# Merge stage of a hybrid decoder block: 11 gates and w_out loaded ahead of the first tiles' stores, parts added by VectorE, next chunk's loads written behind a row block

## The chip, the cores and the metric

One core of a Trainium2 chip runs the whole program. The time is device microseconds of one execution. Engines are named as the profile names them: PE is TensorE (PEld its weight loads), DVE is VectorE, ACT is ScalarE, POOL is GpSimd, and SP is the engine whose queue (SPq) issues most DMAs. ACT issues some as well (ACTq). Each engine takes its instructions strictly in the order in which they stand.

## What is computed

One layer of a decoder block on x (1 x 2048 x 1024, float32): an RMSNorm and a projection into q, k, v, u, z and two gates; dilated windowed attention (`y_attn`, 256 wide) and a chunked spatial gating (`y_gmlp`, 512 wide); a merge; then a squared-ReLU MLP. The change is in the merge. Cut from the reference:

```python
gate_a = jax.nn.sigmoid(proj[..., GA0:GB0])
gate_b = jax.nn.sigmoid(proj[..., GB0:IN_WIDTH])
...
merged = (gate_a * jnp.einsum('bse,ed->bsd', y_attn, w_branch_attn[layer])
          + gate_b * jnp.einsum('bse,ed->bsd', y_gmlp, w_branch_gmlp[layer]))
y = jnp.einsum('bsd,de->bse', merged, w_out[layer])
x = x + _rmsnorm(y, norm_post_mix[layer])
h = _rmsnorm(x, norm_pre_mlp[layer])
```

Every product is made of three float32r products: each operand is split into a rounded part (`hi`) and the rest (`lo`), and hi x hi, hi x lo and lo x hi are summed in PSUM (`mm3`, L94). A split costs one copy by ACT (L70) and one subtraction by DVE (L78).

## The kernel before

**Stages.** The kernel first makes the projections and the attention, then the merge and the output projection, then the MLP. The merge works on four chunks of 512 positions, in the order 2, 3, 0, 1 (L900). Gates, `y_attn` and `y_gmlp` lie in device memory by then (`gate_d`, `ya_d`, `yg_d`), with the channels as rows.

**One merge** (L798) has eight steps `dt` of 128 output channels. Each step takes two gate tiles of 128x512 (g0 for the attention branch, g1 for the gMLP branch): SP loads them (L795), ACT takes the sigmoid in place (L809), PE makes the branch product (6 matmuls for g0, 12 for g1, L95 to L97, tile `b`), DVE multiplies gate and product (L813), POOL adds the two parts (L815; in the last step DVE does), and ACT and DVE split the sum into the tile `mg` (L70, L78). Products use a ring of four PSUM banks: the product of step dt+2 waits until the one of the same branch in step dt has been multiplied away. Gate tiles are rings as well: three for g0, two for g1, so a load of g1 two steps on waits for the sum of this step, and a load of g0 three steps on for its split.

**Output blocks.** After the merge of a chunk come four `out_block`s (L823) of 128 rows: 16 groups of three matmuls with the split w_out (`wo`, eight tiles), then squares, two norms and the residual on ACT and DVE (L852 to L862), and later eight transposes (tile `pt`, L868). The last block's transposes fall into the next chunk's merge, where `flush` asks for them behind step 0 and step 2. In the first block the group of the last merge step (k = 7) is moved to the eleventh place. POOL computes sums of the transposed tiles (`tt`, L873 to L876) for every second chunk.

**What is special in the first merge (chunk 2).** It runs right behind the last projection (tile `z`). `spatial_out` (L1088) is called after each step. In steps 0 and 1 it also runs `sz_out` (L425) for chunks 0 and 1: 16 small matmuls for each of four groups into the second ring of four PSUM banks (tile `sz_cg`, c the chunk, g the group, L430), a DVE instruction into a tile `sb` (L437), a product with `ur`, loaded by SP (L434), on DVE or POOL (L440), and a store of `sb` to `yg_d` by SP (L441). There are three `sb` tiles and two `ur` tiles, so the fourth group waits for the first one's store. In every step it also loads and splits one eighth of w_out (L779 to L781, `woraw`, two tiles), and after the last step it loads the two norm gains (L1099, L1100).

**The order.** Only PE's order is fixed by the code here. The orders of SP, ACT, DVE and POOL are made by a scheduler that draws them up from the order of the code and its own estimates, so that a small edit can move instructions far from it.

Of the kernel before, what the change touches and what calls it, by code (L numbers as in the profile page):

```python
# [8 lines left out]
F32 = mybir.dt.float32  # L9
# [7 lines left out]
P = 128  # L17
S = 2048
D = 1024
KT = 8  # L20
# [11 lines left out]
def bcast(src):  # L32
    return bass.AP(tensor=src.tensor, offset=src.offset, ap=[[0, P], [1, src.shape[-1]]])
# [8 lines left out]
def block_kernel(ctx, tc, a, out):  # L42
# [284 lines left out]
    with ExitStack() as e1a:  # L327
# [40 lines left out]
        for half in range(2):  # L368
# [15 lines left out]
            for n, (g, which) in enumerate(qk):  # L384
                w = nxt
# [383 lines left out]
    e2b, e2 = ExitStack(), ExitStack()  # L769
    bot = stack(e2b, "bot", 1)  # L770
    sm = stack(e2b, "sm2", 2)
    gpost = bot.tile([P, D], F32, name="gpost")
    gmlp = bot.tile([P, D], F32, name="gmlp")
    gtp = stack(e2, "gtp", 2)
    mgp = [stack(e2, "mg0", 1)]
    wop = stack(e2, "wop", 1)
    wo = [wop.tile([P, 2, D], F32R, name=f"wo{k}") for k in range(KT)]

    def load_wo(k):  # L779
        raw = bot.tile([P, D], F32, name=f"woraw{k}", tag="y1", bufs=2)  # L780
        split_in(wo[k], a["w_out"][:, k, :], raw, "act")  # L781

    def load_y(c, engs=("act", "dve")):
        cs = slice(c * 512, (c + 1) * 512)
# [3 lines left out]
        return yt  # L788

    gates = {}  # L790

    def load_gate(c, dt, wch):
        if (c, dt, wch) not in gates:
# [4 lines left out]
    def merge(c, yt, between, each=None):  # L798
        cs = slice(c * 512, (c + 1) * 512)
        mg = []  # L800
        for dt in range(KT):
            dsl = slice(dt * P, (dt + 1) * P)
            if dt % 4 == 0:
                mg.append(mgp[dt // 4].tile([P, 2, 4, 512], F32R, name=f"mg{c}{dt}", tag="mg"))
            parts = []
            for wch, ks in ((0, range(0, 2)), (1, range(2, 6))):
                load_gate(c, dt, wch)
                gt = gates.pop((c, dt, wch))
                act.activation(gt, gt, AF.Sigmoid)  # L809
# [3 lines left out]
                dve.tensor_mul(gt, gt, p)  # L813
                parts.append(gt)
            (dve if dt == KT - 1 else pool).tensor_add(parts[0], parts[0], parts[1])  # L815
# [271 lines left out]

    def spatial_out(dt):  # L1088

        nonlocal ttp  # L1090
        if dt < 2:
            sz_out(*late.pop(0))
        if dt == 1:
            ez.close()
            mgp.append(stack(e2, "mg1", 1))
            ttp = stack(e2r, "ttp", 2, side="right")
        load_wo(dt)
        if dt == KT - 1:
            sp.dma_start(gpost, bcast(a["norm_post_mix"]))  # L1099
            sp.dma_start(gmlp, bcast(a["norm_pre_mlp"]))  # L1100

# [13 lines left out]

    ttp = None
    yt = load_y(2, ("pool", "pool"))
    mg = merge(2, yt, {}, spatial_out)
    for n, c in enumerate(chunks):
        if n:  # L1120
            mg = merge(c, yt, {0: flush, 2: flush, 3: store, 6: store})
        if n < 3:
            yt = load_y(chunks[n + 1])
            for dt in range(2):
                for wch in range(2):
                    load_gate(chunks[n + 1], dt, wch)
# [578 lines left out]
```

## Time and profile before

| | us |
|---|---|
| median of 3 runs | 2776.09 (2775.97 to 2780.45) |
| the profiled execution | 2779.44 |
| its span, first to last instruction | 2777.7 |
| PE busy in the span | 2712.0 |
| merge of chunk 2 on PE (first `b` matmul to first `o` matmul) | 1132.70 to 1182.55 |
| chunk 3, first `o` matmul | 1264.55 |
| chunk 0, first `o` matmul | 1353.35 |

All times inside the span count from its start. A row of the timeline gives start, length, engine, line, operation, output tile <- input tiles, and in brackets the idle time before it and what ended that. A row of the view of waits reads: who waited, for whom, us in total, how often, the longest. A row of the view of windows gives busy us of each engine in a stretch, with the instruction count in parentheses, then the granted PE clock, the share of time the DMA engines were busy, and GB/s. Two matmuls that follow each other overlap in these rows; their pace is the distance of their starts.

### The profile page before, as it was taken

How to read it: one execution, taken by the hardware profiler on the slowest of the kernel's cores; microseconds unless marked ns; L12 is line 12 of the kernel's file. 1: busy time of each engine (PE TensorE's matmuls, PEld its weight loads, DVE VectorE, ACT ScalarE, POOL GpSimd, SP SyncE). 2: the span in 40 equal slices, each digit the busy share in tenths (PEclk: the TensorE clock that was granted, in tenths of full speed). 3: DMA queues.
4: the chain of work that ended last, by engine and by line, in shares of the span. 5: the costliest groups of instructions: out<-in, count | busy, mean ns of one | idle time of the engine just before them, and what ended most of it. 6: DMA issues, size and time to landing. Idle time of an engine off the chain costs nothing. (4 is left out here: it accounts for less than half of the span.)

```text
span 2777.7 us, 34732 instructions
## 1 busy us (share of the span) xinstructions
PE 2712.0 (98%) x12668; PEld 2242.3 (81%) x12668; DVE 1545.2 (56%) x2643; ACT 1051.9 (38%) x2151; POOL 947.3 (34%) x777
## 2 busy tenths in 40 slices
PE   9999999999999999999999999999999999999998
PEld 7888888888878887787787788878887887777787
DVE  5655552344453344554556644555436777777766
ACT  5213111244453321354444544555444333233334
POOL 0341341200000013312215432223314766677645
PEclk9999999999999999999999999999999999999999
DMA  7445455466666654655658534554343122222236
GB/s 266 168 145 169 156 152 195 126 190 195 193 217 192 190 166 149 186 190 160 183 171 268 168 103 125 181 168 126 106 146 108 54 84 84 84 84 84 84 106 213
DMA packets 298380, 426.00 MB, mean 153 GB/s; under 512 B 18528, under 2 KB 172384, under 8 KB 298208
## 3 DMA queue, kind: packets, MB, share of 16 engines
q1 hardware_dynamic: 210368, 372.12, 42.3%
q10 hardware_dynamic: 87840, 51.65, 6.2%
q8 instruction: 100, 1.64, 0.2%
q14 instruction: 72, 0.59, 0.1%
HBM read 282.99 MB, written 140.71 MB: 153 GB/s over the span
## 5 line engine op out<-in xcount | busy, mean ns | idle before, releaser
L1556 PE MATMUL ya<-T_spots,s 128*128 128x512 f32 x1272 | 313.1, 392 | 4.8 <-DVE acc L1564 2.7
L1556 PEld LDWEIGHTS ya<-T_spots,s 128*128 128x128 f32 x1272 | 239.0, 188 | 59.0 <-issue 4.5
L70 ACT ACTIVATE s<-sraw 128x768 fp32r<-128x768 f32 (+1 forms) x184 | 126.0, 695 | 358.2 <-POOL sraw L1355 199.0
L1016 PE MATMUL aa<-B,A 128*128 128x512 f32 x768 | 187.0, 396 | 6.3 <-ACT xs L1030 5.1
L78 DVE TENSOR_TENSOR s<-sraw,s 128x512 fp32r<-128x512 f32 x171 | 163.6, 979 | 34.6 <-ACT s L70 33.0
L987 POOL TENSOR_TENSOR s<-w1r 128x512 f32<-128x512 f32 x32 | 43.5, 1359 | 397.3 <-DVE S L78 337.3
L1016 PEld LDWEIGHTS aa<-B,A 128*128 128x128 f32 x768 | 145.5, 190 | 40.5 <-ACT xs L1030 6.0
L72 POOL TENSOR_SCALAR w_g<-w_g_r 128x1024 fp32r<-128x1024 f32 x32 | 34.1, 1082 | 412.3 <-PE g L97 313.7
L1556 PE MATMUL yc<-T_spots,s 128*128 128x512 f32 x624 | 164.1, 394 | 3.6 <-POOL T_spots L78 3.6
L95 PE MATMUL x<-hT_a,wq 128*128 128x512 f32 x384 | 149.7, 390 | 0.0
L97 PE MATMUL x<-hT_a,wq 128*128 128x512 f32 x384 | 149.4, 389 | 0.0
L96 PE MATMUL x<-hT_a,wq 128*128 128x512 f32 x384 | 149.4, 389 | 0.0
L1556 PEld LDWEIGHTS yc<-T_spots,s 128*128 128x128 f32 x624 | 115.8, 188 | 33.6 <-POOL T_spots L78 9.7
L653 DVE TENSOR_REDUCE o<-po 128x256 f32<-128x512 f32 x48 | 33.1, 690 | 187.5 <-PE po L652 187.5
L78 POOL TENSOR_TENSOR T_spots<-w2r,T_spots 128x512 fp32r<-128x512 f32 x86 | 123.2, 1459 | 5.4 <-ACT T_spots L70 5.4
L70 ACT ACTIVATE hl<-r 128x512 fp32r<-128x512 f32 x48 | 30.4, 633 | 233.2 <-POOL r L287 89.0
L95 PE MATMUL g<-hT_b,w_g 128*128 128x512 f32 x256 | 105.0, 410 | 0.0
L95 PE MATMUL g<-hT_a,w_g 128*128 128x512 f32 x256 | 104.8, 409 | 0.0
L95 PE MATMUL o<-wo,mg 128*128 128x512 f32 x256 | 100.8, 394 | 4.1 <-ACT mg L70 4.1
L70 ACT ACTIVATE S<-w1r 128x512 fp32r<-128x512 f32 x96 | 60.0, 629 | 112.0 <-PE ac L1016 66.6
L815 POOL TENSOR_TENSOR g<-g,g 128x512 f32<-128x512 f32 x28 | 38.8, 1385 | 185.9 <-DVE g L813 179.2
L1354 POOL TENSOR_TENSOR sraw<-sraw 128x256 f32<-128x256 f32 x56 | 41.3, 737 | 174.6 <-DVE s L78 160.3
(379 smaller groups left out, 7214.4 us busy)
## 6 DMA issues: line engine op xcount, KB each, us to landing
w1r<-in_w_mlp_in_dram SPq DMA_DIRECT2D x64, 512.0 KB, 3.6
sraw<-sd SPq DMA_DIRECT2D x128, 256.0 KB, 3.4
qk<-hl SPq DMA_DIRECT2D x24, 1024.0 KB, 5.4
qq<-qk SPq DMA_DIRECT2D x96, 256.0 KB, 5.1
w_g_r<-in_w_in_dram SPq DMA_DIRECT2D x32, 512.0 KB, 5.3
gated<-gt SPq DMA_DIRECT2D x64, 256.0 KB, 3.4
g<-gated SPq DMA_DIRECT2D x64, 256.0 KB, 4.4
w2r<-in_w_mlp_out_dram SPq DMA_DIRECT2D x16, 1024.0 KB, 6.0
```

The source lines that it names most:

```text
L70: act.activation(hi, src, AF.Copy)
L72: pool.tensor_scalar(hi, src, 1.0, 1.0, op0=OP.mult, op1=OP.mult)
L78: (pool if lo_eng == "pool" else dve).tensor_sub(lo, src, f32(hi))
L95: pe.matmul(ps, lh, rh, start=start, stop=False)
L96: pe.matmul(ps, lh, rl, start=False, stop=False)
L97: pe.matmul(ps, ll, rh, start=False, stop=stop)
L653: dve.tensor_reduce(ot[:, :, j * 64:(j + 1) * 64], po.rearrange("p (b h e) -> p b e h", b=4, h=2), axis=AX.X, op=OP.add)
L815: (dve if dt == KT - 1 else pool).tensor_add(parts[0], parts[0], parts[1])
L987: pool.tensor_add(s1, a21, a22)
L1016: pe.matmul(p, w[:, l, k, :], h[:, r, k, :], start=i in (1, 6, 5) and not k and not n, stop=k == 3 and n == 2, skip_group_check=True)
L1354: pool.tensor_add(a22, a21, a22)
L1556: pe.matmul(p, s[:, l], w[:, r], start=i in (1, 2, 5) and not m and not o, stop=m == 1 and o == 2, skip_group_check=True)
```

## The change

Four edits, all in the merge stage:

1. A new function `early_gates` stands ahead of the first merge. It writes the loads of 11 of the 16 gates of chunk 2, with the first two w_out loads among them. Six of the gates go into tiles that belong to later users (the x rows of an output block and the two norm gains); five go into the usual rings. The gains' tiles are taken only at the end of that merge.
2. w_out is loaded two steps ahead: load and split are separate, and a split asks for the load two tiles on.
3. The two parts of a step are added by DVE in every step, instead of by POOL in seven of eight.
4. The loads of the next chunk's `yt` and of its first four gates stand behind the first output block in the code, instead of ahead of it.

```diff
-    gpost = bot.tile([P, D], F32, name="gpost")
-    gmlp = bot.tile([P, D], F32, name="gmlp")
+    gpost = gmlp = None
...
     def load_wo(k):
-        raw = bot.tile([P, D], F32, name=f"woraw{k}", tag="y1", bufs=2)
-        split_in(wo[k], a["w_out"][:, k, :], raw, "act")
+        wo_raw[k] = bot.tile([P, D], F32, name=f"woraw{k}", tag="y1", bufs=2)
+        sp.dma_start(wo_raw[k], a["w_out"][:, k, :])
+
+    def split_wo(k):
+        split(wo[k][:, 0], wo[k][:, 1], wo_raw.pop(k))
+        if k + 2 < KT:
+            load_wo(k + 2)
...
+    def early_gates(c):
+
+        w = [bot.tile([P, D], F32, name=f"gates{n}", tag=t) for n, t in enumerate(("xr", "gpost", "gmlp"))]
+        places = [z[:, h * 512:(h + 1) * 512] for z in w for h in range(2)]
+        for n in range(11):
+            dt, wch = n // 2, n % 2
+            if n < 6:
+                gates[c, dt, wch] = places[n]
+                sp.dma_start(places[n], gate_d[wch * 8 + dt, :, c * 512:(c + 1) * 512])
+            else:
+                load_gate(c, dt, wch)
+            if n in (1, 3):
+                load_wo(n // 2)
...
-            (dve if dt == KT - 1 else pool).tensor_add(parts[0], parts[0], parts[1])
+            dve.tensor_add(parts[0], parts[0], parts[1])
...
-        load_wo(dt)
+        split_wo(dt)
         if dt == KT - 1:
+            gpost = bot.tile([P, D], F32, name="gpost")
+            gmlp = bot.tile([P, D], F32, name="gmlp")
...
     yt = load_y(2, ("pool", "pool"))
+    early_gates(2)
     mg = merge(2, yt, {}, spatial_out)
...
-        if n < 3:
-            yt = load_y(chunks[n + 1])
-            for dt in range(2):
-                for wch in range(2):
-                    load_gate(chunks[n + 1], dt, wch)
         for i in range(4):
             store()
             b = out_block(c, i, mg, flush_older)
             next(b)
             last.append(b)
+            if n < 3 and not i:
+                yt = load_y(chunks[n + 1])
+                for dt in range(2):
+                    for wch in range(2):
+                        load_gate(chunks[n + 1], dt, wch)
```

What the scheduler makes of it is seen in the orders. First SP's queue at the start of the first merge, right behind the loads of `yt` for chunk 2. Before (`g0_20` is the gate of branch 0, chunk 2, step 0; `sb_01` belongs to chunk 0, group 1):

```order
L795 DMA g0_20_9526<-gated_73 128x512
L795 DMA g1_20_9537<-gated_73 128x512
L91 DMA woraw0_9601<-in_w_out_dram 128x1024
L795 DMA g0_21_9605<-gated_73 128x512
L795 DMA g1_21_9616<-gated_73 128x512
L91 DMA woraw1_9687<-in_w_out_dram 128x1024
L795 DMA g0_22_9691<-gated_73 128x512
L795 DMA g1_22_9702<-gated_73 128x512
L441 DMA ygd_78<-sb_00_9562 128x512
L441 DMA ygd_78<-sb_01_9573 128x512
L434 DMA ur_02_9585<-ud_72 128x512
L434 DMA ur_03_9596<-ud_72 128x512
```

The same place now (`gates0` holds both gates of step 0, `gates1` those of step 1, `gates2` those of step 2):

```order
L807 DMA gates0_9523<-gated_73 128x512 x2
L783 DMA woraw0_9528<-in_w_out_dram 128x1024
L807 DMA gates1_9524<-gated_73 128x512 x2
L783 DMA woraw1_9532<-in_w_out_dram 128x1024
L807 DMA gates2_9525<-gated_73 128x512 x2
L816 DMA g0_23_9536<-gated_73 128x512
L816 DMA g1_23_9538<-gated_73 128x512
L816 DMA g0_24_9540<-gated_73 128x512
L816 DMA g1_24_9542<-gated_73 128x512
L816 DMA g0_25_9544<-gated_73 128x512
L441 DMA ygd_78<-sb_00_9579 128x512
L441 DMA ygd_78<-sb_01_9590 128x512
```

Five gates (`g0_23` to `g0_25`) have moved ahead of the first stores. In the built program the first two gates wait for nothing on PE any more; `woraw0` now waits for the last `z` matmul instead.

Second DVE in the same merge, from the subtraction for w_out tile 2 on. Before:

```order
L78 TENSOR_TENSOR wo2_9495<-woraw2_9722,wo2_9495 128x1024
L437 SCALAR_TENSOR_TENSOR sb_12_9663<-sz_12_9658,lngb0_9117,bsp0_9116 128x512
L440 TENSOR_TENSOR sb_11_9652<-sb_11_9652,ur_11_9653 128x512
L813 TENSOR_TENSOR g0_22_9691<-g0_22_9691,b0_22_9694 128x512
L437 SCALAR_TENSOR_TENSOR sb_13_9674<-sz_13_9669,lngb0_9117,bsp0_9116 128x512
L813 TENSOR_TENSOR g1_22_9702<-g1_22_9702,b1_22_9705 128x512
L813 TENSOR_TENSOR g0_23_9726<-g0_23_9726,b0_23_9729 128x512
```

The same stretch now, from one row earlier:

```order
L834 TENSOR_TENSOR gates2_9525<-gates2_9525,b0_22_9705 128x512
L437 SCALAR_TENSOR_TENSOR sb_11_9665<-sz_11_9660,lngb0_9117,bsp0_9116 128x512
L78 TENSOR_TENSOR wo2_9493<-woraw2_9620,wo2_9493 128x1024
L437 SCALAR_TENSOR_TENSOR sb_12_9676<-sz_12_9671,lngb0_9117,bsp0_9116 128x512
L440 TENSOR_TENSOR sb_11_9665<-sb_11_9665,ur_11_9666 128x512
L834 TENSOR_TENSOR gates2_9525<-gates2_9525,b1_22_9714 128x512
L834 TENSOR_TENSOR g0_23_9536<-g0_23_9536,b0_23_9736 128x512
L836 TENSOR_TENSOR gates2_9525<-gates2_9525 128x512
L437 SCALAR_TENSOR_TENSOR sb_13_9687<-sz_13_9682,lngb0_9117,bsp0_9116 128x512
L834 TENSOR_TENSOR g1_23_9538<-g1_23_9538,b1_23_9745 128x512
```

The multiplication for `b0_22` has moved ahead of four instructions, those for `b1_22` and `b0_23` ahead of `sb_13`, and each sum of parts (L836) is new on DVE.

Third DVE in the merge of chunk 0, where the last output block of chunk 3 (row block 33) is finished. Before:

```order
L105 RECIPROCAL r_post33_10972<-r_post33_10972 128x1
L108 SCALAR_TENSOR_TENSOR t_post33_10977<-r_post33_10972,v_post33_10974 128x1
L112 TENSOR_SCALAR t_post33_10977<-t_post33_10977 128x1
L113 TENSOR_TENSOR r_post33_10972<-r_post33_10972,t_post33_10977 128x1
L857 SCALAR_TENSOR_TENSOR xr_33_10891<-y1_33_10963,r_post33_10972,xr_33_10891 128x1024
L78 TENSOR_TENSOR mg00_10995<-g0_00_10602,mg00_10995 128x512
L813 TENSOR_TENSOR g0_01_10606<-g0_01_10606,b0_01_11040 128x512
```

Now:

```order
L105 RECIPROCAL r_post33_10969<-r_post33_10969 128x1
L836 TENSOR_TENSOR g0_00_10687<-g0_00_10687,g1_00_10689 128x512
L108 SCALAR_TENSOR_TENSOR t_post33_10974<-r_post33_10969,v_post33_10971 128x1
L112 TENSOR_SCALAR t_post33_10974<-t_post33_10974 128x1
L113 TENSOR_TENSOR r_post33_10969<-r_post33_10969,t_post33_10974 128x1
L834 TENSOR_TENSOR g0_01_10691<-g0_01_10691,b0_01_11037 128x512
L878 SCALAR_TENSOR_TENSOR xr_33_10888<-y1_33_10960,r_post33_10969,xr_33_10888 128x1024
L78 TENSOR_TENSOR mg00_10992<-g0_00_10687,mg00_10992 128x512
```

A sum and a multiplication now stand ahead of the residual `xr_33`, and behind it another sum (of `g0_01` and `g1_01`) stands between `xr_33` and the last norm of that row block. PE's order is the same in both kernels. In the orders of SP, ACT and DVE the loads and splits of `yt` for chunks 3, 0 and 1 stand where they stood; of edit 4 there is only this to see: the x rows of the first output block are loaded ahead of `yt` for chunk 3, and one square of that block stands ahead of one sigmoid.

More of the change, by code (lines that the diff above doesn't have):

```diff
@@ L777, in block_kernel @@
     wo = [wop.tile([P, 2, D], F32R, name=f"wo{k}") for k in range(KT)]
+    wo_raw = {}
     def load_wo(k):
-        raw = bot.tile([P, D], F32, name=f"woraw{k}", tag="y1", bufs=2)
-        split_in(wo[k], a["w_out"][:, k, :], raw, "act")
+        wo_raw[k] = bot.tile([P, D], F32, name=f"woraw{k}", tag="y1", bufs=2)
[4 more added lines that the diff above has]
+            load_wo(k + 2)
     def load_y(c, engs=("act", "dve")):
@@ L1088, in spatial_out @@
     def spatial_out(dt):
-        nonlocal ttp
+        nonlocal ttp, gpost, gmlp
         if dt < 2:
```

## Prediction

> **What bounds the kernel now.** The page first: its span and PE's line.
>
> ```profile
> span 2777.7 us, 34732 instructions
> PE 2712.0 (98%) x12668; PEld 2242.3 (81%) x12668; DVE 1545.2 (56%) x2643; ACT 1051.9 (38%) x2151; POOL 947.3 (34%) x777
> ```
>
> PE is busy in all but 65.7 us, and the change takes no matmul away. It can bring only time in which PE waits, or in which it runs at a lower clock, and only in the merge stage. So the view of PE's waits from 1090 to 1500 us comes next, then PE's busy time and clock in the first merge and in a short piece of it.
>
> ```profile
> PE b L95 <- DVE g L813: 6.0, 5, 1.9
> PE o L95 <- ACT mg L70: 4.1, 4, 2.1
> PE pt L868 <- ACT g L809: 3.4, 1, 3.4
> ```
>
> ```profile
> 1132.70:1182.50 49.80, 43.78 (x209) 34.83 (x208) 32.52 (x50) 22.41 (x32) 15.95 (x10) 0.97 0.77 231
> 1173.90:1177.60 3.70, 3.70 (x9) 2.93 (x10) 2.82 (x4) 3.21 (x5) 1.28 (x1) 0.54 0.61 199
> ```
>
> Five waits in the first merge make 6.0 us, and behind the last of them nine matmuls run at 0.54 of the clock. The timeline of PE gives the rest: the two lots of small matmuls, the pace, the first and the last of the five waits, the first `o` matmul, and the wait in the first output block.
>
> ```profile
> 1136.90 3.73 PE L430 MATMUL sz<-wsp,z 128*128 128x128 f32 x32
> ...
> 1144.67 3.96 PE L430 MATMUL sz<-wsp,z 128*128 128x128 f32 x32
> ...
> 1148.71 0.39 PE L96 MATMUL b<-yt,wb 128*128 128x512 f32 x1
> ...
> 1156.64 0.40 PE L97 MATMUL b<-yt,wb 128*128 128x512 f32 x1
> 1158.12 0.51 PE L95 MATMUL b<-yt,wb 128*128 128x512 f32 x1 [1.08 <-DVE g L813]
> ...
> 1173.89 0.55 PE L95 MATMUL b<-yt,wb 128*128 128x512 f32 x1 [1.89 <-DVE g L813]
> ...
> 1182.55 0.42 PE L95 MATMUL o<-wo,mg 128*128 128x512 f32 x1
> ...
> 1190.16 0.50 PE L95 MATMUL o<-wo,mg 128*128 128x512 f32 x1 [0.59 <-ACT mg L70]
> ```
>
> From 1148.71 to 1156.64 there are 34 steps of a matmul, 0.233 us each. The merge has 8 x 18 = 144 matmuls: 33.6 us. The small ones take 3.73 and 3.96 us less an overlap of 0.23 each: 7.2 us. Together 40.8 us, but from 1132.70 to 1182.55 pass 49.85. **Lost: 9.05 us.** Of that 6.0 is the waits; 3.7 - 9 x 0.233 = 1.6 is the low clock; the other 1.4 is 0.28 at each of the five restarts. The wait at 1190.16 costs 0.59 + 0.28 = 0.87 more. So 9.9 us are lost up to there.
>
> Why DVE was late is read from its own timeline, and why the gates were, from SP's.
>
> ```profile
> 1155.68 0.75 DVE L437 SCALAR_TENSOR_TENSOR sb<-sz,lngb,bsp 128x512 f32<-128x512 f32 x1
> 1156.35 1.12 DVE L440 TENSOR_TENSOR sb<-sb,ur 128x512 f32<-128x512 f32 x1
> 1157.39 0.67 DVE L813 TENSOR_TENSOR g<-g,b 128x512 f32<-128x512 f32 x1
> 1160.09 0.75 DVE L437 SCALAR_TENSOR_TENSOR sb<-sz,lngb,bsp 128x512 f32<-128x512 f32 x1 [2.02 <-DMA ygd<-sb]
> 1160.75 1.28 DVE L813 TENSOR_TENSOR g<-g,b 128x512 f32<-128x512 f32 x2
> ```
>
> ```profile
> 1132.89 0.79 SPq L795 DMA_DIRECT2D g<-gated  x2
> ...
> 1142.39 1.88 SPq L441 DMA_DIRECT2D ygd<-sb  x2
> 1144.31 0.92 SPq L434 DMA_DIRECT2D ur<-ud  x2
> ...
> 1152.12 0.41 SPq L795 DMA_DIRECT2D g<-gated  x1
> ```
>
> The first wait ends with the multiplication of 1157.39, which stands behind two instructions of the `sz` chain. The next, at 1160.75, stands behind a 2.02 us wait for a store. The later ones follow gates of step 3 on, which SP could issue only at 1152.12 and after, since stores that wait for POOL or DVE stand ahead of them.
>
> **The change part by part.** *Early gates and the new DVE order (edits 1 and 2).* No DMA is added; 13 loads (11 gates of 128x512 float32, two of w_out of twice that) now precede the first store. The first two gates leave SP earlier, behind the loads of `yt`; the other 3.4 MB start at 1132.9 as before, at some 0.4 us an issue (0.79 for two). What the DMA engines move there is in the windows:
>
> ```profile
> 1133.50:1137.50 4.00, 4.00 (x22) 3.32 (x21) 3.24 (x11) 3.49 (x4) 0.00 (x0) 1.00 0.72 138
> 1137.50:1143.50 6.00, 6.00 (x42) 5.41 (x41) 4.05 (x8) 3.48 (x6) 2.53 (x2) 1.00 0.96 339
> ```
>
> 0.55 MB go in the slow first 4 us, the other 2.85 MB at 339 GB/s take 8.4 us: all landed at about 1146. The gate of step 5 is wanted by its multiplication at 1163, so gates up to g0 of step 5 no longer hold PE. Behind them the stores and `ur` loads wait in line. How long those take here (from issue to landing, least, median, most) is in the views of `ur`, of `sb` and of the gates, in this order:
>
> ```profile
> DMA to landing us min/median/max: 3.6/4.1/4.7
> ```
>
> ```profile
> DMA to landing us min/median/max: 2.4/3.7/4.5
> ```
>
> ```profile
> DMA to landing us min/median/max: 3.5/4.9/8.5
> ```
>
> I carried the new DVE order through by hand with 0.6 us for each 128x512 instruction (two took 1.28), 1.2 for each w_out subtraction, and 5 us from issue to landing, the gates' median, since the same bytes now go in less time. The first store leaves at 1141.3 (1142.39 before, behind a sum on POOL), so `sb_03` comes at about 1147.9; PE reaches `sz_13` at 1147.4 and **waits some 0.5 to 1 us** there. Then the multiplications for `b0_22`, `b1_22`, `b0_23` and `b1_23` end near 1151, 1157, 1157 and 1159; PE needs their banks at 1158, 1159, 1162 and 1163. None waits. The tail is tighter: w_out tiles 5, 6, 7 and gates 6 and 7 wait for DVE to free their places. The split of step 7 ends near 1180, and PE asks for it 6.7 us after its first `o` matmul, at about 1181. I leave 1.5 us for what is late at both places. **Term A: -9.9 + 1.5 = -8.4 us.** If no wait is left it is -9.9; the other end is the rivals below.
>
> *The clock.* I let the 1.6 us go with the waits, since 0.54 is the only low clock of that stage and stands right behind them. The Trainium skill speaks against this: "TensorE: Matmul & The Clock Gate", section "What's actually happening", has the clock halve after an idle window of about 3.4 us, and the longest wait here is 1.89 us. By that rule the low clock would have another cause and stay, and term A would be -6.8. The trace differs from the rule at this place: it shows the drop after a wait of 1.89 us.
>
> *Sums on DVE (edit 3).* Seven sums per chunk leave POOL. Where PE waits for a chunk's last splits, at the start of chunk 3's output blocks, they are in the path:
>
> ```profile
> 1269.73 0.50 PE L95 MATMUL o<-wo,mg 128*128 128x512 f32 x1 [0.90 <-ACT mg L70]
> ...
> 1273.53 0.50 PE L95 MATMUL o<-wo,mg 128*128 128x512 f32 x1 [0.51 <-ACT mg L70]
> ...
> 1274.67 0.50 PE L97 MATMUL o<-wo,mg 128*128 128x512 f32 x1 [0.41 <-DVE mg L78]
> ```
>
> ```profile
> L815 POOL TENSOR_TENSOR g<-g,g 128x512 f32<-128x512 f32 x6 | 9.1, 1517 | 25.4 <-DVE g L813 25.4
> ```
>
> A sum takes 1.3 to 2.2 us on POOL (mean 1.517); the DVE multiplication of the same shape took 0.67. A place in the ring of gates comes free about 0.65 us sooner, and with it the last gate. The three waits hold 1.82 us and 0.84 of restarts. **Term B: -1.2 us**, between 0 and -2.7; I take the middle, since the last split also stands behind splits of `yt`, which stay.
>
> In chunk 0's merge the sums go the other way. Here are POOL, DVE, and PE's two waits of that chunk:
>
> ```profile
> 1318.40 1.29 POOL L873 TENSOR_TENSOR tt<-tt 128x512 f32<-128x512 f32 x1 [3.39 <-ACT tt L869]
> 1319.64 1.29 POOL L815 TENSOR_TENSOR g<-g,g 128x512 f32<-128x512 f32 x1
> ```
>
> ```profile
> 1318.74 0.97 DVE L108 SCALAR_TENSOR_TENSOR t_post<-r_post,v_post 128x1 f32<-128x1 f32 x1
> ...
> 1319.93 1.02 DVE L113 TENSOR_TENSOR r_post<-r_post,t_post 128x1 f32<-128x1 f32 x1
> ...
> 1320.99 2.28 DVE L857 SCALAR_TENSOR_TENSOR xr<-y,r_post,xr 128x1024 f32<-128x1024 f32 x1
> ```
>
> ```profile
> 1329.91 1.06 PE L868 MATMUL pt<-ident,y 128*128 128x128 f32 x8 [3.38 <-ACT g L809]
> ```
>
> ```profile
> 1362.42 0.50 PE L95 MATMUL o<-wo,mg 128*128 128x512 f32 x1 [2.08 <-ACT mg L70]
> ```
>
> Instructions of one element per row last 0.97 and 1.02 us: they end when POOL's do, so DVE and POOL take turns. The sum of step 0 is another such turn, and the multiplication moved ahead of `xr` adds 0.6. `xr` is ready later, by 1.3 to 2.4 us; behind it POOL has one instruction less in the way, and two DVE instructions stand differently. I get the last norm of row block 33, for which PE waits at 1329.91, 1.2 us later. **Term C: +1.2 us**, between -1.3 (one POOL sum gone) and +2.6 (two turns of 1.29). The 2.08 us at 1362.42 stay: that split stands behind splits of `yt` that wait for their loads.
>
> *Next chunk's loads behind a row block (edit 4).* The orders hardly change, so: 0. The gains and x rows that come earlier are covered by 40 us of `o` matmuls.
>
> **Sum.** -8.4 - 1.2 + 1.2 = -8.4 us. The profiled execution took 2779.44 us (span 2777.7 and 1.7 around it), 3.35 above the median of 2776.09; it would become 2771.0. What is behind is bound by PE and moves along, so the median becomes **2767.7 us**.
>
> **Rivals.** *One wait for another.* If landings take 6.5 us and not 5, the chain load of `ur`, product, store, next `sb` runs late, DVE's strict order passes it on, and I get waits of 1.1 us at `sz_13`, 1.9 at `b0_26` and 3.7 at the first `o` matmul, where the bank is freed behind w_out tile 6. 6.7 of the 9.9 are given back: 2776.1 - 3.2 = 2772.9 us. For it: the gates' 8.5 us at most, and 3.4 MB in line. Against it: `ur` and `sb` never took over 4.7.
>
> *Slower.* With 8.5 us for every landing the same chain makes waits of 2.9 (`sz_13`), 1.9 (`b1_24`), 3.9 (`b0_26`) and, for w_out tile 7, whose load waits for tile 5, 5.0: 13.7 where 9.9 were. That is +3.8: 2779.9 us. It decides from landings of about 7.7 us on. Against it: 8.5 came only in the first burst.
>
> *It doesn't do what it says.* If the scheduler's order makes the gates early but the multiplications as late as before, PE gains nothing: 2776.1 us. The order speaks against it: `b0_22` is ahead of four instructions, `b1_22` and `b0_23` ahead of the one that waited for a store.
>
> **How the numbers follow.** My forecast and what lies about it (2762.2 to 2770.5): 0.70. One wait for another: 0.15. No gain: 0.05. Slower: 0.10. A measurement of this kernel tells 0.2%, 5.6 us, from no change; so faster (below 2770.5) is 0.70. The slower rival's 2779.9 lies within 0.2%, and passes 2781.6 where landings take more than 8.5 us; I give that 0.06 of its 0.10. So same is 0.15 + 0.05 + 0.04 = 0.24, slower 0.06. The low end is all best ends together: -9.9 - 2.7 - 1.3 = -13.9, 2762.2. The high end, 2775, takes in the first rival with term C at +2.6 and leaves out the slower one.
>
> **What would show it.** In the profile after, the first `o` matmul stands at about 1175 and the five waits on L813 are gone or one short wait at `sz` has replaced them; no clock under 0.9 between 1132 and 1190. Chunk 3's three waits are about half. The wait for `pt` in chunk 0 is no shorter. Wrong would be: landings over 6 us for `ur` and `sb`, with waits at `b0_26` or at the first `o` matmuls; or a low clock without a wait.

## The result, and the profile after

The changed kernel is a little faster: 0.9983 of the time before, with an interval of 0.9978 to 0.9989 (medians 2774.18 and 2779.88 us, 22 executions of each). Of 2779.88 the ratio makes 4.7 us, between 3.1 and 6.1; the medians lie 5.7 apart. The forecast was 8.4 us. The direction was right, the gain is a little over half of what was forecast. The forecast also started too low: its 2776.09 was the median of three executions, and of 22 it is 2779.88, so that the profiled execution of before (2779.44) stands at the median and not 3.35 us above it.

The two profiled executions stand 8.9 us apart, more than the medians do: the one of the changed kernel, 2770.54 us, is among the shortest of its 22 (2769.63 to 2781.85). So the comparison below goes by places. From the page of the changed kernel:

```profile
span 2768.8 us, 34666 instructions
PE 2708.5 (98%) x12668; PEld 2242.7 (81%) x12668; DVE 1561.6 (56%) x2671; ACT 1052.5 (38%) x2151; POOL 907.5 (33%) x749
```

28 instructions have gone from POOL to DVE: the seven sums of four chunks. The view of PE's waits from 1090 to 1500 us:

```profile
PE pt L889 <- DVE y L883: 4.7, 1, 4.7
PE o L95 <- ACT mg L70: 2.5, 2, 2.2
PE sz L430 <- DVE sb L437: 1.9, 1, 1.9
PE o L97 <- DVE mg L78: 0.4, 1, 0.4
...
```

The five waits for a multiplication of gates (6.0 us) are gone. In their place stands one of 1.9 us at `sz`, and the wait for `pt` in chunk 0 has grown from 3.4 to 4.7. PE's timeline shows where they stand:

```profile
1136.17 3.73 PE L430 MATMUL sz<-wsp,z 128*128 128x128 f32 x32
...
1148.68 1.15 PE L430 MATMUL sz<-wsp,z 128*128 128x128 f32 x8 [1.90 <-DVE sb L437]
...
1176.41 0.40 PE L95 MATMUL o<-wo,mg 128*128 128x512 f32 x1
...
1264.36 0.50 PE L95 MATMUL o<-wo,mg 128*128 128x512 f32 x1 [0.25 <-ACT mg L70]
1265.51 0.50 PE L97 MATMUL o<-wo,mg 128*128 128x512 f32 x1 [0.41 <-DVE mg L78]
...
1322.07 1.94 PE L889 MATMUL pt<-ident,y 128*128 128x128 f32 x8 [4.69 <-DVE y L883]
...
1355.55 0.50 PE L95 MATMUL o<-wo,mg 128*128 128x512 f32 x1 [2.22 <-ACT mg L70]
```

The measure for the first merge is the distance from the first `sz` matmul to the first `o` matmul, since both executions reach that stage at slightly different times (1136.90 and 1136.17). It went from 45.65 to 40.24 us. The wait at `sz` costs more than its 1.90 us. The windows of 3.41 us around it:

```profile
1146.26:1149.67 3.41, 1.51 (x14) 1.35 (x13) 2.13 (x4) 1.90 (x4) 0.53 (x1) 1.00 0.74 273
1149.67:1153.08 3.41, 3.41 (x11) 2.64 (x10) 1.95 (x4) 1.06 (x1) 0.75 (x1) 0.50 0.48 142
1153.08:1156.49 3.41, 3.41 (x16) 2.77 (x15) 2.96 (x5) 0.00 (x0) 1.77 (x1) 1.00 0.93 326
```

Behind the wait PE runs one stretch of 3.41 us at half its clock, which costs up to 1.7 us (half of 3.41). The wait itself is explained on DVE, on SP and by the view of the tile `sb`:

```profile
1147.79 0.75 DVE L437 SCALAR_TENSOR_TENSOR sb<-sz,lngb,bsp 128x512 f32<-128x512 f32 x1 [1.28 <-DMA ygd<-sb]
```

```profile
1140.98 1.68 SPq L441 DMA_DIRECT2D ygd<-sb  x2
```

```profile
DMA to landing us min/median/max: 2.3/4.0/6.7
```

The fourth `sb` waits for the first one's store. That store was issued at 1140.98, behind 11 gates and two w_out loads, and took 6.7 us (the longest; before, none took over 4.5). DVE was done with its earlier work at 1146.5 and stood still for 1.28 us until it landed.

### The profile page after: what moved, and what is told of

Read it like the earlier page. It is cut to its first block, busy times and chain, and to the rows that moved or that the text cites. A ratio compares the mean times of both kernels' runs of the same rounds, so it can differ in the third digit from the quotient of the medians.

```text
span 2768.8 us, 34666 instructions
## 1 busy us (share of the span) xinstructions
PE 2708.5 (98%) x12668; PEld 2242.7 (81%) x12668; DVE 1561.6 (56%) x2671; ACT 1052.5 (38%) x2151; POOL 907.5 (33%) x749
## 5 line engine op out<-in xcount | busy, mean ns | idle before, releaser
L95 PE MATMUL g<-hT_a,w_g 128*128 128x512 f32 x256 | 104.8, 410 | 0.0
L95 PE MATMUL o<-wo,mg 128*128 128x512 f32 x256 | 100.5, 393 | 2.5 <-ACT mg L70 2.5
L97 PE MATMUL g<-hT_a,w_g 128*128 128x512 f32 x256 | 100.8, 394 | 0.0
L97 PE MATMUL o<-wo,mg 128*128 128x512 f32 x256 | 100.0, 391 | 0.5 <-DVE mg L78 0.4
```

Source lines behind the costliest of these rows:

```text
L95: pe.matmul(ps, lh, rh, start=start, stop=False)
L97: pe.matmul(ps, ll, rh, start=False, stop=stop)
```

## The experiments

All ratios are to the kernel before, run on the same chip as the kernel in question. "Merge" below is the distance from the first `sz` to the first `o` matmul in the profiled execution.

| kernel | merge, us | waits of PE in it, us | ratio, 95% interval |
|---|---|---|---|
| before | 45.65 | 1.08, 1.71, 0.33, 1.02, 1.89 (`b`) | 1 |
| changed | 40.24 | 1.90 (`sz`) | 0.9983 (0.9978 to 0.9989) |
| sums on POOL again | 41.41 | 3.17 (`sz`) | 0.9990 (0.9981 to 0.9999) |
| before, sums on DVE | 44.87 | 1.53 (`sz`), 2.47, 1.20 (`b`), 0.64 (`o`) | 1.0002 (0.9993 to 1.0011) |
| fourth `sb` | 41.12 | 1.02, 0.65 (`b`), 2.22 (`o`) | 0.9988 (0.9979 to 0.9996) |
| loads ahead | 40.22 | 1.88 (`sz`) | 0.9986 (0.9977 to 0.9995) |
| stores from ACT | 44.26 | 2.35 (`sz`), 1.20, 0.22, 1.33 (`b`) | 1.0003 (0.9994 to 1.0012) |
| 7 early gates | 42.04 | 3.70 (`b`) | 0.9990 (0.9981 to 0.9999) |
| fourth `sb`, two w_out loads | 37.64 | 0.85 (`b`) | 0.9972 (0.9960 to 0.9983) |
| fourth `sb`, low parts on POOL | 42.17 | 3.82 (`b`) | 0.9991 (0.9982 to 1.0000) |
| first transposes later | 41.27 | 2.83 (`sz`) | 0.9970 (0.9959 to 0.9980) |
| stores from ACT, first transposes later | 43.40 | 1.26 (`sz`), 2.67, 0.59, 1.27 (`b`) | 0.9971 (0.9959 to 0.9982) |
| both transposes later | 40.45 | 1.84 (`sz`), 1.67 (`o`) | 0.9964 (0.9952 to 0.9977) |
| both transposes later, 9 early gates | 39.99 | 2.72 (`b`) | 0.9959 (0.9945 to 0.9973) |

The table also shows how far a single profile can be trusted. The changed kernel and the runs "loads ahead", "first transposes later" and "both transposes later" have the same orders of PE, DVE, ACT and POOL in this merge, and it took 40.24, 40.22, 41.27 and 40.45 us; the two runs with stores from ACT, also alike there, took 44.26 and 43.40. Differences of about 1 us between two rows are not told apart by these profiles.

**The sums apart from the rest.** First the changed kernel with the sums back on POOL, then the kernel before with the sums alone on DVE:

```diff
-            dve.tensor_add(parts[0], parts[0], parts[1])
+            (dve if dt == KT - 1 else pool).tensor_add(parts[0], parts[0], parts[1])
```

> The changed kernel with the seven sums of a chunk back on POOL (edits 1, 2 and 4 stay). Theory 1 (nearly all of the gain comes from the early gates, and the sums on DVE bring in chunk 3 about what they cost in chunk 0): ratio to the kernel before 0.9983, within 0.0006; the wait for pt in chunk 0 back at about 3.4 us (4.7 in the changed kernel), chunk 3's three short waits back at about 1.8 us in all (0.7). Rival (the sums on DVE eat the missing part of the gain): ratio 0.9976 or less, by 2 us or more.

> The kernel before with edit 3 alone: all sums of parts on DVE. Theory 1: ratio 1.0000, within 0.0005; the waits for a multiplication of gates in the first merge stay near 6.0 us, with a low clock behind them; pt in chunk 0 about 4.7 us. Rival: the sums cost in chunk 0 more than they bring: 1.0007 or more. A third way (the sums free places in the ring of gates also in the first merge and are a part of the gain): 0.9993 or less, with the five waits shorter by 2 us.

PE's timeline with the sums on POOL, and with the sums alone:

```profile
1152.28 2.04 PE L430 MATMUL sz<-wsp,z 128*128 128x128 f32 x8 [3.17 <-DVE sb L437]
```

```profile
1325.70 1.59 PE L889 MATMUL pt<-ident,y 128*128 128x128 f32 x8 [3.37 <-DVE y L883]
```

```profile
1330.69 1.94 PE L868 MATMUL pt<-ident,y 128*128 128x128 f32 x8 [5.07 <-DVE y L862]
```

The ratio with the sums alone (1.0002) lies where theory 1 put it; that with the sums on POOL (0.9990) lies just outside the 0.0006 that it allowed, on the other side than its rival. The intervals are wide (2.5 us to each side), so the profiles have to carry the sizes. Term C is confirmed on both kernels: the wait for `pt` is 3.37 and 3.38 us with the sums on POOL, and 4.69 to 5.07 in the eight profiles with the sums on DVE and the transposes in their old place. The first merge is 1.2 us shorter with the sums on DVE and early gates (41.41 to 40.24) and 0.8 without (45.65 to 44.87), but equal orders differ by 1.05, so a help there isn't shown. The three waits at chunk 3's output blocks are 1.35 us in all with the sums on POOL and 0.66 in the changed kernel, where 1.8 and 0.7 were expected; yet in the twelve profiles with the sums on DVE they lie between 0 and 1.41, so one pair doesn't give the size. Without the early gates two waits for a multiplication remain, of 3.7 us in all, and the low clock behind one of them: so edits 1 and 2 carry most of the gain in the merge (44.87 to 40.24).

**A fourth place for `sb`.**

```diff
-            t = zp.tile([P, 512], F32, name=f"sb_{c}{g}", tag="sz", bufs=2 if c > 1 else 3)
+            t = zp.tile([P, 512], F32, name=f"sb_{c}{g}", tag="sz", bufs=2 if c > 1 else 4)
```

> The changed kernel with a fourth place for the products sb in the first merge, so that the fourth one of chunk 0 needn't wait for the first one's store to land. Theory 1 (the missing gain is the 1.9 us wait at the last eight small matmuls, the low clock of some 1.6 us behind it and 0.28 for the restart, all from that store's 6.7 us): the wait is gone, no clock under 0.9 between 1140 and 1182, the first o matmul some 3.8 us earlier, ratio 0.9969 (2.6 to 4.5 us less than the changed kernel). Rival (one wait for another: the products and gates behind it are late anyway and PE waits at a later bank): ratio 0.9980 to 0.9984, with a new wait of 1 to 3 us between 1149 and 1182.

```profile
1167.42 0.50 PE L95 MATMUL b<-yt,wb 128*128 128x512 f32 x1 [1.02 <-DVE g L834]
...
1179.22 0.47 PE L95 MATMUL o<-wo,mg 128*128 128x512 f32 x1 [2.22 <-DVE g L834]
1185.79 0.50 PE L95 MATMUL o<-wo,mg 128*128 128x512 f32 x1 [2.24 <-ACT mg L70]
```

The rival's case. The wait at `sz` is gone and so is the low clock, and the merge is no shorter for it (41.12): PE waits for later banks instead, and 2.24 us more in the first output block. The five gates issued behind the first stores land in 6.5 us (median, 8.2 at most), against 5.2 in the changed kernel. The edit does more than it says: the scheduler also drew up other orders for DVE, ACT and SP. Theory 1 falls in that form: taking away that one wait doesn't bring the missing gain.

**Edit 4 undone.** The next chunk's loads are written ahead of the first row block again.

> The changed kernel with edit 4 undone: the next chunk's loads and gates are written ahead of the first row block again. Theory 1 (edit 4 is worth nothing): ratio 0.9983, within 0.0005, the same waits at the start of chunk 3's and chunk 0's output blocks within 0.4 us. Rival (the later place of the loads makes the splits of yt late and eats part of the gain): 0.9978 or less. The other side (it is a part of the gain, since the x rows and the gains come first): 0.9988 or more.

Ratio 0.9986 where 0.9983 was expected, the merge 40.22 against 40.24. Edit 4 is worth nothing that can be measured. Chunk 3's output blocks start without the two short waits (0.25 and 0.41) here, but so they do in the run with both lots of transposes later, which has edit 4.

**Stores from another queue, and fewer gates.** Two ways to get the first store through sooner:

```diff
-            sp.dma_start(yg_d[g, :, c * 512:(c + 1) * 512], t)
+            (sp if c > 1 else act).dma_start(yg_d[g, :, c * 512:(c + 1) * 512], t)
```

```diff
-        for n in range(11):
+        for n in range(7):
```

> The changed kernel with the eight stores of the products sb in the first merge issued by ACT and not by SP, so that they stand in another queue than the gates. Theory 1 (the first store took 6.7 us to land because it stood in line behind 11 gates, and SP, which waits for each product before it can issue, held up the w_out loads and the late gates): the first store lands within 5 us, the wait at the last small matmuls is under 0.7 us, from the first small matmul to the first o matmul pass 38 to 39 us (40.24 in the changed kernel, 45.65 before), ratio 0.9976. Rival A (the DMA engines are full whatever the queue, 285 GB/s in that stretch): landing 6 us or more, 40 us, ratio 0.9983. Rival B (ACT now waits for products and its sigmoids come late): 41 us or more, 0.9988.

> The changed kernel with 7 gates ahead of the first stores and not 11 (1 MB less in line). Theory 1: the first store lands within 5.5 us and the wait at the last small matmuls is under 0.9 us, but the gates of steps 4 on are late again and PE waits there for 1 to 3 us: ratio 0.9983 to 0.9990. Rival (the gates beyond the seventh aren't needed that early): no new wait, 38 to 39 us from the first small matmul to the first o matmul, ratio 0.9976 or less.

DVE with the stores from ACT, then PE with seven gates:

```profile
1148.14 0.75 DVE L437 SCALAR_TENSOR_TENSOR sb<-sz,lngb,bsp 128x512 f32<-128x512 f32 x1 [5.59 <-DMA ygd<-sb]
```

```profile
1164.75 0.50 PE L95 MATMUL b<-yt,wb 128*128 128x512 f32 x1 [3.70 <-DVE g L834]
```

From ACT the first store is issued at 1140.78 and the `sb` that waits for it starts at 1148.14, 7.4 us later: the queue that it stands in is not what holds it up. The Trainium skill says so ("DMA: Bandwidth & Descriptors", section "Issuing engines are not separate DMA queues": queues of different engines share the same 16 DMA engines), and this run agrees. The merge is 4 us longer (44.26). The scheduler has put DVE's order together differently (DVE stands still for 5.59 us here), and some of ACT's splits now stand behind stores; which of the two costs more is open. That part was rival B; rivals A and B were both half right. With seven gates the wait at `sz` is gone, PE waits 3.7 us for the first gate that isn't loaded early (g1 of step 3), and the ratio is 0.9990: about theory 1's numbers, with a longer wait than its 1 to 3 us. The first store shows what it stands behind: it lands 2.6 us after its issue with seven gates ahead, 4.4 with nine (the last run below), and 6.6 to 7.7 with eleven in the seven profiles in which SP issues it and DVE subtracts the low parts.

**Is it the transfers or DVE?** Theory 2 came from these runs. The window of the changed kernel's merge:

```profile
1136.17:1176.41 40.24, 38.34 (x192) 32.03 (x191) 34.42 (x49) 19.50 (x29) 6.02 (x4) 0.96 0.86 285
```

At 285 GB/s some 11.5 MB pass in these 40 us, so theory 2 is that whatever is put ahead makes something else late. The rival is DVE, which is busy for 34.4 of them. ACT and DVE in the run with the fourth `sb`, ahead of the 2.22 us wait at its first `o` matmul:

```profile
1172.53 0.63 ACT L830 ACTIVATE g<-g 128x512 f32<-128x512 f32 x1 [5.48 <-DMA g<-gated]
```

```profile
1173.19 0.69 DVE L834 TENSOR_TENSOR g<-g,b 128x512 f32<-128x512 f32 x1 [2.89 <-ACT g L830]
...
1178.39 0.68 DVE L834 TENSOR_TENSOR g<-g,b 128x512 f32<-128x512 f32 x1
```

Both have a part in it. DVE stands still for 2.89 us, since ACT waits for a gate to land; the multiplication that frees PE's bank then stands behind three instructions that came late with it, though its own gate was ready at 1176.07. Two runs were to part them. Both kernels have the fourth `sb`, so that the wait at `sz` doesn't hide what is behind it.

```diff
         split(wo[k][:, 0], wo[k][:, 1], wo_raw.pop(k))
-        if k + 2 < KT:
-            load_wo(k + 2)
...
+        split(wo[k][:, 0], wo[k][:, 1], wo_raw[k % 2])
```

```diff
-        split(wo[k][:, 0], wo[k][:, 1], wo_raw.pop(k))
+        split(wo[k][:, 0], wo[k][:, 1], wo_raw.pop(k), lo_eng="pool")
```

> The kernel with the fourth place for sb, and in it only two of the eight w_out tiles are loaded; the other six are split from those two, so that 3.1 MB of loads in the first merge are left out with their waits (the output is then not the reference's). Theory 2 (in the first merge what PE waits for next is bounded by the transfers: some 11.5 MB at 285 GB/s): the late gates land in 5.5 us or less (8.2 with all loads), no wait over 0.5 us from the first small matmul to the first o matmul, which takes 37 to 38.5 us (41.1 with all loads, 40.2 in the changed kernel). Rival (the order and the load of DVE bound it, its work is the same here): 40 us or more, with the same waits for a multiplication of gates.

> The kernel with the fourth place for sb, and the eight low parts of w_out subtracted by POOL and not by DVE, which takes some 9.7 us of work from DVE in the first merge. Theory 2 (transfers): from the first small matmul to the first o matmul 40.5 us or more, the late gates land in 7 us or more. Rival (DVE): 39 us or less, the waits for a multiplication of gates under 1 us in all.

PE without six of the loads, and with the low parts on POOL:

```profile
1159.89 0.50 PE L95 MATMUL b<-yt,wb 128*128 128x512 f32 x1 [0.85 <-DVE gates L832]
...
1175.39 0.40 PE L95 MATMUL o<-wo,mg 128*128 128x512 f32 x1
```

```profile
1174.66 0.50 PE L95 MATMUL b<-yt,wb 128*128 128x512 f32 x1 [3.82 <-DVE g L834]
```

Without six w_out loads the merge takes 37.64 us with the same work on DVE, and the five late gates land in 3.6 us (median; 6.5 with all loads. The 8.2 of the expectation counts gates of the first burst too). That agrees with theory 2, but for one wait of 0.85 us that it did not allow. The run takes away the bytes, the waits for the two `woraw` tiles and six places in SP's queue together; which of the three counts most is open. The other run isn't as clean as it was meant: POOL needs 2.4 us for a subtraction that DVE does in 1.2, frees the `woraw` tiles later, and makes DVE take turns (a sum of 0.68 us lasts 2.78). Its 42.17 us lie where theory 2 put them, but its late gates land in 4.2 us (median) and not in 7 or more: PE's 3.82 us come from a w_out load, for which ACT stands still 3.33 us ahead of the split of a sum, and from a turn with POOL (a subtraction of 0.68 us lasts 2.42). So this run doesn't part the two, and that the transfers alone bound the merge is argued, not shown.

**The wait for `pt` in chunk 0.** Two lots of transposes are asked for in that merge: those of row block 32 behind step 0, those of row block 33, for which PE waits, behind step 2. First the former one step later, then the same with the stores from ACT, then both lots later, and then this with nine early gates:

```diff
-            mg = merge(c, yt, {0: flush, 2: flush, 3: store, 6: store})
+            mg = merge(c, yt, {int(n == 2): flush, 2: flush, 3: store, 6: store})
```

```diff
-            mg = merge(c, yt, {0: flush, 2: flush, 3: store, 6: store})
+            mg = merge(c, yt, {2: flush, 3: flush, 4: store, 6: store} if n == 2 else {0: flush, 2: flush, 3: store, 6: store})
```

> The changed kernel with the transposes of row block 33 in chunk 0's merge one step later (behind the 18 matmuls of step 1, 4.2 us). Theory 1 (the sums on DVE made y of that row block 1.3 us late, term C, and the whole wait of 4.7 us with the low clock behind it is there only because the transposes stand right behind step 0): the wait for pt is under 1 us, no low clock near 1320, 4 to 6 us less than the changed kernel, ratio 0.9965. Rival (what is behind the transposes, the subtractions on POOL and the loads of the next chunk, is then late in its turn): the wait goes but 2 us or more come back between 1325 and 1520; ratio 0.9976 or more.

> Both of the two edits before: stores from ACT, and the transposes one step later. Theory 1: the two gains add up, since they are 150 us apart: ratio 0.9958. If either brings nothing by itself, the other's ratio.

The first expectation names the wrong lot: the edit moves the transposes of row block 32, and the wait stands behind step 2. It shows something else for that. DVE and POOL in the changed kernel, then DVE and POOL with the first lot one step later:

```profile
1309.47 1.62 DVE L836 TENSOR_TENSOR g<-g,g 128x512 f32<-128x512 f32 x1
1311.01 1.25 DVE L108 SCALAR_TENSOR_TENSOR t_post<-r_post,v_post 128x1 f32<-128x1 f32 x1
1312.30 0.15 DVE L112 TENSOR_SCALAR t_post<-t_post 128x1 f32<-128x1 f32 x1
1312.48 1.02 DVE L113 TENSOR_TENSOR r_post<-r_post,t_post 128x1 f32<-128x1 f32 x1
1313.43 0.67 DVE L834 TENSOR_TENSOR g<-g,b 128x512 f32<-128x512 f32 x1
1314.03 1.80 DVE L878 SCALAR_TENSOR_TENSOR xr<-y,r_post,xr 128x1024 f32<-128x1024 f32 x1
```

```profile
1309.25 1.29 POOL L894 TENSOR_TENSOR tt<-tt 128x512 f32<-128x512 f32 x1 [3.38 <-ACT tt L890]
1310.62 1.62 POOL L895 TENSOR_TENSOR tt<-tt 128x512 f32<-128x512 f32 x1
1312.21 1.28 POOL L896 TENSOR_TENSOR tt<-tt 128x512 f32<-128x512 f32 x1
1313.46 1.28 POOL L897 TENSOR_TENSOR tt<-tt 128x512 f32<-128x512 f32 x1
```

```profile
1311.56 0.68 DVE L836 TENSOR_TENSOR g<-g,g 128x512 f32<-128x512 f32 x1
1312.15 0.21 DVE L108 SCALAR_TENSOR_TENSOR t_post<-r_post,v_post 128x1 f32<-128x1 f32 x1
...
1313.73 1.29 DVE L878 SCALAR_TENSOR_TENSOR xr<-y,r_post,xr 128x1024 f32<-128x1024 f32 x1
```

```profile
1316.13 1.46 POOL L894 TENSOR_TENSOR tt<-tt 128x512 f32<-128x512 f32 x1 [7.60 <-ACT tt L890]
```

In the changed kernel the four subtractions on POOL (`tt`; the section on the kernel calls them sums) behind row block 32's transposes run beside row block 33's norm on DVE, and DVE's instructions with two inputs in SBUF get through only when one of POOL's ends: the sum 1.62 us, `t_post` 1.25, `xr` 1.80. The other step of `t_post` (L112), with one input tensor (0.15), and the multiplication with `b`, which lies in PSUM (0.67), are not held up. One step later POOL is silent at that time, and the same three take 0.68, 0.21 and 1.29. But that isn't the whole difference. ACT in the changed kernel, then the last instruction of the norm on DVE with the first lot one step later:

```profile
1315.87 3.08 ACTq L881 DMA_DIRECT2D x1d<-xr  x1
...
1318.99 0.29 ACT L102 ACTIVATE r_pm<-s,edge 128x1 f32<-128x1 f32 x1 [1.98 <-issue]
```

```profile
1320.30 2.25 DVE L883 SCALAR_TENSOR_TENSOR y<-xr,r_pm,gmlp 128x1024 f32<-128x1024 f32 x1
```

ACT stores `xr` ahead of the second norm, and issuing that DMA takes 3.08 us here, so that `r_pm` comes 1.98 us late. In the eight profiles with the sums on DVE and the transposes in their old place the issue takes 3.1 to 3.5 us, in the other six 0.33; why isn't shown. And POOL's subtractions, moved, now meet the end of the norm (`y` 2.25 for 1.28). The chain that ends with `y`, from the start of `v_post` (L104) on, in us:

| | to the end of `xr` | on to the start of `r_pm` on DVE | on to the end of `y` | sum | wait for `pt` |
|---|---|---|---|---|---|
| before | 5.37 | 2.88 | 3.61 | 11.86 | 3.38 |
| changed | 7.09 | 3.49 | 2.60 | 13.18 | 4.69 |
| first lot one step later | 3.60 | 2.88 | 4.65 | 11.13 | 2.63 |

The differences of the sums are those of the waits. (Before and with the first lot later the profile names an ACT instruction for the wait; it ended 0.1 us behind `y`.) The wait for `pt` falls to 2.63, the 2.22 us wait at the start of chunk 0's output blocks goes, and the ratio is 0.9970 (0.9959 to 0.9980). With the stores from ACT added it is 0.9971 (0.9959 to 0.9982): nothing added, as that edit brought nothing alone.

> The changed kernel with both lots of transposes in chunk 0's merge moved: those of row block 32 from step 0 to step 2, those of row block 33 (for which PE waits) from step 2 to step 3. In the run with the first lot one step later the wait fell from 4.7 to 2.6 us, since POOL's four subtractions behind the first lot no longer ran beside DVE's chain of row block 33. Theory 3 (the wait is that chain, made late by turns with POOL, and PE arriving too early): no wait for pt over 0.5 us, and 2 to 3 us less than in that run: ratio 0.9960. Rival (the subtractions, stores and loads that come later hold up chunk 0's output blocks or the start of the MLP): a new wait of 2 us or more, ratio 0.9970 or more.

> As the run before, and with 9 gates ahead of the first stores instead of 11. With 11 the fourth sb waits for a store that takes 6.7 us, with 7 that wait is gone but a gate of step 4 is 3.7 us late. Theory 2 (both are the same transfers in one line): at 9 both waits shrink but neither goes, 39 to 40.5 us from the first small matmul to the first o matmul, ratio within 0.0005 of the run before. Rival (there is a place between where neither waits): 38.5 us or less, and 1.5 to 3 us less than the run before.

PE with both lots later, then with nine gates in addition:

```profile
1316.31 1.03 PE L889 MATMUL pt<-ident,y 128*128 128x128 f32 x8
1321.39 1.03 PE L889 MATMUL pt<-ident,y 128*128 128x128 f32 x8
```

```profile
1169.62 0.50 PE L95 MATMUL b<-yt,wb 128*128 128x512 f32 x1 [2.72 <-DVE g L834]
```

No wait for `pt` is left. Shorter ones come at the start of chunk 0's output blocks (0.97, 0.98 and 0.41 in the first, 1.01, 1.91 and 0.41 in the second). The ratios are 0.9964 (0.9952 to 0.9977) and 0.9959 (0.9945 to 0.9973), medians of 2769.54 and 2767.99 us: both beat the kernel before by 10 to 11 us and the changed one by some 5 to 7. Theory 3 holds for the wait; the gain over the run with the first lot alone (0.9970) is 1.7 us by the ratios, where 2 to 3 were expected, and within the intervals. Between 9 and 11 gates no difference can be told; the merge takes 39.99 and 40.45 us, in the first with one wait of 2.72, in the second with 1.84 at `sz` and 1.67 at the first `o`. At nine the wait at `sz` is gone, which theory 2 had not expected, and a later one has come; at none of the three numbers tried does PE run through.

## Why the prediction was right or wrong

**What bounds the kernel: right.** Nearly all that can be followed was gained or lost in PE's waits and in its clock, at the places named; 0.7 us has no name (see the sum).

**Term A (early gates and DVE's order): right in mechanism, too large.** Forecast -8.4, measured -5.4 in the merge and -0.87 for the wait at 1190.16, which is gone: -6.3. (In the run with the same merge and a wait of 2.83 it would be 1 us less.) The failed step is "waits some 0.5 to 1 us there" with the 1.5 us that were left for both late places. The place was right, and so was PE's arrival: 1146.78, which is 1147.5 in the times of before (this execution reached the stage 0.73 earlier), where 1147.4 had been worked out. But `sb_03` starts at 1148.5 in those times and not at 1147.9, and it has to end too, 0.75 later. So the wait is 1.90, and a restart (0.28) and a low clock (1.7) belong to it. That is 3.9 us where 1.5 stood (by the distance, 9.9 - 6.3 = 3.6).

Two things were mis-sized. The clock behind the remaining wait had no price. And the 5 us for each landing were a median; the one store on which the step hangs took 6.7, since the burst ahead of it landed late: the last of the 11 gates at 1147.04 (1147.8 in the times of before, where about 1146 had been worked out), the store 0.65 behind it. With 5 us DVE would have come to `sb_03` at 1147.2 in those times, when its earlier work was done, and PE would have waited some 0.5 us (an estimate from these rows). The forecast's own 1141.3 + 5 makes 1146.3; what it put between that and its 1147.9 it doesn't say, and the store left 0.4 later than it had it, so that its "0.5 to 1" is not as close as it looks.

What came out is the first half of the rival "one wait for another", which had 6.5 us: a wait at `sz_13`, without its later waits: only the first two stores took over 6 us (6.7 and 6.0), the other six 2.3 to 5.1. So of what the prediction said would show it wrong, landings over 6 us came, and the waits at `b0_26` and at the first `o` matmul did not. The run with the fourth `sb` shows those later waits to be next in line, and with six w_out loads (3.1 MB) left out they shrink to one of 0.85 us. I had looked at DVE's order and at the single landing, not at the sum of bytes: the stage moves 285 GB/s on average with 86% of the DMA engines' time, so what is put ahead puts something else back: the first store by about 2 us for each two gates.

**The clock: the low clock did follow the wait, and that is why it was not gone.** "No clock under 0.9 between 1132 and 1190" failed with the wait. Of the two readings, that the 1.6 us go with the waits and that they have another cause, the runs bear out the first: with the fourth `sb` and with nine gates the merge has no low clock at all, and in all 14 profiles each low stretch between 1140 and 1420 us stands behind a stretch in which PE waited, or behind another low one in which it did.

**Term B: right in sign, its size partly luck.** Forecast -1.2. The three waits of 1.82 us have become two of 0.66 in all, with one restart less: -1.4. But other profiles with the sums on DVE have between 0 and 1.41 us there, and the one with the sums on POOL 1.35; the share of the sums in this isn't shown.

**Term C: right, with two costs that were not in it.** Forecast +1.2, measured 4.69 - 3.38 = +1.3: `xr` comes 1.7 us later, as worked out (1.3 to 2.4), the end of the norm runs 1.0 faster with POOL out of the way, and 0.6 comes from ACT's long issue, which was not foreseen. The longer wait also costs clock: two stretches at half clock instead of one, of which 5.09 us fall on running matmuls (before 3.41), another 0.84 us. From `pt` to the first wait of chunk 0's output blocks the changed kernel takes 33.48 us and the one before 32.51, 0.97 more. The 2.08 us there stayed, as forecast (2.22).

**Edit 4 at 0: right.**

**The sum.** -5.4 (merge), -3.0 (first `o` matmul to PE's arrival at `pt`, 143.98 to 140.97: the wait at 1190, term B, and 0.7 that I can't name), +1.3, +1.0: -6.1 by the profiles at chunk 0's output blocks. That is the upper end of the interval of 3.1 to 6.1. Of the other 2.8 us between the two profiled spans (8.9) 0.7 stand ahead of the first merge and 2.0 behind chunk 0's first output block; the 4.7 us of the ratio leave no room for them.

## What to carry to other kernels

Before loads are moved forward, add up the bytes of the stage and hold them against what its DMA engines move: here, at 86% busy, loads put ahead made a store late, and another queue didn't help; leaving out 3.1 MB did. A wait must be priced with the clock behind it. Where two engines take turns, look at what the off-path one runs during the chain that is late, and at DMA issues that stand in that chain: moving two lots of transposes, and POOL's subtractions with them, by two steps and by one brought about as much as the whole change. And profile equal code more than once before a difference of 1 us is given a cause.

## What the runs showed of the hardware

The low clock comes in fixed stretches. In each profile it starts and ends on a grid of 3.413 us that runs on from the start: in the kernel before, stretches begin at 1174.21 and 1331.22, which are 46.0 steps apart, in the changed one at 1149.67 and 1320.33, 50.0 steps apart. The windows of before at two of them and of the changed kernel at the one behind `pt`:

```profile
1170.80:1174.21 3.41, 1.52 (x7) 0.94 (x6) 0.69 (x1) 1.15 (x2) 0.29 (x1) 1.00 0.97 353
1174.21:1177.62 3.41, 3.41 (x9) 2.64 (x8) 2.84 (x4) 2.92 (x5) 0.99 (x1) 0.50 0.57 181
...
1331.22:1334.63 3.41, 3.41 (x9) 2.65 (x9) 0.69 (x1) 2.31 (x5) 2.19 (x2) 0.50 1.00 323
```

```profile
1320.33:1327.16 6.83, 5.09 (x16) 4.41 (x17) 2.85 (x5) 3.01 (x5) 0.00 (x0) 0.50 0.71 219
```

In the 14 profiles, between 1140 and 1420 us, a stretch in which PE had waited for 1.88 us or more was always followed by one at half clock (1.88, 1.89, 1.90 the shortest), and a stretch at full clock with less than 1.65 us of waiting never was. In between both occur: 1.75 to 1.84 in one stretch lowered nothing five times, and 1.65 to 1.81, each in two pieces, did four times (1.24 and 0.41 the least). In a stretch that was itself low, 0.86 and 1.00 were enough for another low one. A wait of 2.72 that fell on two stretches (0.90 and 1.82) lowered nothing. So it is the idle share of a fixed stretch, at about half, that decides (what exactly is counted these rows don't show), and the same wait costs up to 1.7 us more or nothing depending on where it falls. The Trainium skill ("TensorE: Matmul & The Clock Gate", section "What's actually happening") has the free-running window of 3413 ns, which these rows agree with; it asks for a whole idle window, and here 1.88 us of one was enough. As the grid starts elsewhere in each execution, this should be part of the spread of 12 us between executions of one kernel; the profiles of single executions can't show how much.
